# Picking by due time in the list schedule of a hybrid gMLP and attention layer

## The chip, the core and the metric

The kernel runs on one core of a Trainium2 chip. The metric is the device time of one launch in microseconds (us). Of the core's engines five matter here: the tensor engine (PE), the vector engine (DVE), the scalar engine (ACT), GpSimd (POOL), and SyncE (SP), which issues most of the DMAs. Each engine works through a list of its own in order; a semaphore makes it wait where an instruction needs what another engine or a DMA makes.

## What is computed

One layer of a streaming encoder, for two groups of tokens with the same weights: 2048 prompt tokens, and 8 running streams of 16 tokens each with 1024 cached keys and values. The width is 1024, with 4 gMLP groups and 4 attention heads of 128.

```
z = rms_norm(x, norm_g) @ w_in
u_a, v_a, g_a, q, k, v, g_b = split(z)
y_a = u_a * (tril(W_s) @ rms_norm(v_a) + b_s) * silu(g_a)      # in chunks of 128 positions
q, k = rms_norm(q), rms_norm(k)                                # two halves of 64 per head
s = q k^T / 8 - slope * |q_pos - k_pos|, block-causal with blocks of 64
o = (softmax(s of half 1) - lam * softmax(s of half 2)) @ v
y_b = rms_norm(o) * 0.8 * silu(g_b)
x = x + concat(y_a, y_b) @ w_out
```

Outputs are `x` of both groups, the new keys and values, and `v_a` of the running streams. All is float32. A product is made of three matmuls: each operand is split into a high part, rounded to a shorter format by a copy on ACT, and a low part, the difference, on DVE or POOL (`split`, line 457; `mm3`, line 469).

## The kernel before

The work has three stretches, which overlap. In the first, to about 943 us of the span, the input projection runs over blocks of weights (`stream`, line 749): for each kind and head, eight weight tiles `w` are loaded, scaled and split (`load_w`, line 608), and multiplied with the transposed tokens `xT` into PSUM accumulators `acc` (`project`, line 636). Behind each accumulator stand the copies and norms of its kind: `vo` (line 681), `z` and `qk` (656 to 674), `sg` and `usg` (688 to 701), `va`, `vn`, `vhl`, `ya` (713 to 743). They leave for DRAM. Attention of the running streams (`sample_scores`, `sample_values`) and of the first half of the prompt (`attention_a`) are woven between. In the second stretch the attention of the second half of the prompt runs together with the output projection `oo` (`out_stream`, line 1285), and in the third the last tiles of the output projection.

In attention, `score_steps` (line 869) makes scores `S` on PE, biases and reduces them on DVE (`ex`, line 889), takes the exponential on ACT (line 893) and joins both halves on DVE (line 905) or on ACT and POOL (908, 909). `value_steps` (line 913) transposes `ex` (`a_tp`), splits it (`aT`) and multiplies with `v` (`oT`). The rotated copies of the queries are made by DMAs from POOL's queue (`qT`, lines 856 and 857).

The program order written so far is not the order in which the engines work. At the end `Order(tc).run()` (line 1340) goes over all instructions and fixes each engine's list:

- `depend` (line 118) finds for each instruction which earlier ones it needs; `buffers` (line 144) finds which tiles share a buffer.
- `cost` (line 188) gives two times in ns for an instruction: until its result is there, and until its engine is free for the next.
- `port` (line 217) marks the instructions of DVE that can't run beside one of POOL.
- `run` (line 229) then plays the program on a clock of its own. An instruction becomes ready when all that it needs is done, plus a reach and a slack for the engine that waits (`SLACK`, `OTHER`, lines 68 and 69); a DMA is done after `FETCH` and its transfer. Whenever an engine is free, it takes of its ready instructions the one with the lowest number, that is, the earliest in program order (lines 321 to 330). Tiles that share a buffer keep their program order.
- What comes out (line 372) is an order per engine, for the DMA issues of SP and POOL as well. On the chip each engine follows this order and starts each instruction when its data is there.

Program order follows the use on PE: the generators yield after each few matmuls, and `weave` (line 1198) alternates them by PE time. The steps behind an accumulator stand right behind its last matmul, although what they make may be needed much later; weights stand where their load is begun.

Of the kernel before, what the change touches and what calls it, by code (L numbers as in the profile page):

```python
# [59 lines left out]
class Order:  # L60
# [4 lines left out]
    PE, ACT, DVE, POOL, SP = (mybir.EngineType.PE, mybir.EngineType.Activation, mybir.EngineType.DVE,  # L65
                              mybir.EngineType.Pool, mybir.EngineType.SP)

    SLACK = {PE: 180.0, SP: 300.0}
    OTHER, FETCH = 50.0, 2300.0

    class Node:
        def __init__(self, ins, idx):
# [115 lines left out]
    def cost(self, n):  # L188

        kind = type(n.ins).__name__[4:]  # L190
        size = max([math.prod([k for s, k in a.ap[1:]]) for a in n.reads + n.writes] or [1])
        accum = len(n.writes) > 1
        if n.dma:
            return 0.0, 560.0 if n.engine == self.POOL else 400.0
        if n.engine == self.PE:
            size = math.prod([k for s, k in n.writes[0].ap[1:]])
            t = 109.0 if size <= P else 4 + 0.4455 * size
            return t + 165, t
        if n.engine == self.ACT:
            t = 165 + 0.83 * size if kind == "TensorCopy" else 205 + 0.835 * size  # L200
            return (t + 190, t + 90) if accum else (t, t - 105)
        if n.engine == self.DVE:
            t = {"TensorTensor": 160 + 1.04 * size, "TensorReduce": 160 + 1.03 * size, "Memset": 100 + 0.5 * size,
                 "Reciprocal": 162.0}.get(kind, 205 + 1.04 * size)
            if size == 1:
                return (270.0, 190.0) if kind == "TensorScalarPtr" else (165.0, 90.0)
            if kind == "TensorScalarPtr" and not n.ins.is_scalar_tensor_tensor:
                t = 170 + 0.56 * size
            return (t + 100, t - 40) if accum else (t, t - 85)
        if kind == "Memset":  # L210
            return 100 + 0.83 * size, 100 + 0.83 * size
        if "pow" in str(n.ins):
            return 300 + 200.0 * size, 250 + 200.0 * size
        t = 190 + 2.16 * size if kind == "TensorTensor" else 195 + 1.1 * size
        return t, t - 50

    def port(self, n):

# [7 lines left out]
        large = math.prod([k for s, k in n.writes[0].ap[1:]]) >= 512 and type(n.ins).__name__ == "InstTensorScalarPtr"  # L226
        return int(len(wide) > 1 or (len(wide) == 1 and large and not psum))

    def run(self):
        N = self.nodes  # L230
        reach = {self.PE: 54.0, self.POOL: 80.0, self.SP: 27.0}
        for n in N:
            n.wait = len(n.deps)
            for d in n.deps:
                N[d].after.append(n.idx)
# [17 lines left out]
        for g in self.gates:  # L253
            for i in g[1]:
                gate[i].append(g)
            for i in g[2]:
                N[i].wait += 1
        cost = [self.cost(n) for n in N]
        ready = [0.0] * len(N)
        left = {k: len(q) for k, q in self.queue.items()}  # L260
        users = {x: len(self.uses[x]) for x in self.tag}
        last, slot, taken, freed = {}, {}, set(), {}
        free = {e: 0.0 for e in (self.POOL, self.DVE, self.ACT, self.PE, self.SP)}
        later, now_, turn, held = {e: [] for e in free}, {e: [] for e in free}, {e: [] for e in free}, set()
        port, busy = [self.port(n) for n in N], [0.0, 0.0, 0.0]
# [21 lines left out]
        def arrive(i):  # L287
            if N[i].new:
                held.add(i)
            else:  # L290
                heapq.heappush(later[N[i].engine], (ready[i], i))

        def place():
            for i in sorted(held):
                got = buffer(i)
                if got:
                    for name, s in got[1]:
                        taken.add(s)
                        slot[name] = s
                        left[s[0]] -= 1  # L300
                    ready[i] = max(ready[i], got[0])
                    held.discard(i)
                    heapq.heappush(later[N[i].engine], (ready[i], i))
                    return True
            return False
# [7 lines left out]
        while left_over:  # L313
            t, e = None, None
            for x in free:
                lock = busy[2 if x == self.DVE else 1]
                for y in ((free[x],) if now_[x] else ()) + ((max(free[x], lock),) if turn[x] else ()) + (
                        (max(free[x], later[x][0][0]),) if later[x] else ()):
                    if t is None or y < t:
                        t, e = y, x  # L320
            while later[e] and later[e][0][0] <= t:
                i = heapq.heappop(later[e])[1]
                heapq.heappush((turn if port[i] else now_)[e], i)
            lock = busy[2 if e == self.DVE else 1]
            if turn[e] and lock <= t and (not now_[e] or turn[e][0] < now_[e][0]):
                i = heapq.heappop(turn[e])
            elif now_[e]:
                i = heapq.heappop(now_[e])
            else:
                continue  # L330
            left_over -= 1
            n = N[i]
            out[e].append(i)
            if n.dma:
                size = 4 * math.prod([k for s, k in n.writes[0].ap])
                dma = max(t + self.FETCH, dma) + max(size / 280, 60.0)
                end = dma + 200
            else:
                end = t + cost[i][0]
            free[e] = t + cost[i][1]  # L340
            if port[i]:
                busy[port[i]] = free[e]
            for j in n.after:
                b = N[j].engine
                if b == e and not n.dma and not N[j].dma:
                    r = free[e]
                else:
                    r = end + reach.get(b, 35.0) + (self.SLACK.get(b, self.OTHER) if b != e or n.dma else 0)
                ready[j] = max(ready[j], r)
                N[j].wait -= 1  # L350
                if not N[j].wait:
                    arrive(j)
            more = list(first[i])
            for g in gate[i]:
                g[0] -= 1
                if not g[0]:
                    more += g[2]
            for j in more:
                ready[j] = max(ready[j], t)
                N[j].wait -= 1  # L360
                if not N[j].wait:
                    arrive(j)
            for name in n.tiles:
                if name in users:
                    last[name] = max(last.get(name, 0.0), end + 35)
                    users[name] -= 1
                    if not users[name]:
                        taken.discard(slot[name])
                        freed[slot[name]] = last[name]
            while held and place():  # L370
                pass
# [7 lines left out]
def trunk_step_kernel(  # L379
# [588 lines left out]
    def attention(sb, sl, groups, wmax, nk, nv, nex, comb, eng):  # L968
# [31 lines left out]
        for i, (key, j) in enumerate(units):  # L1000
# [33 lines left out]
            for _, run in sorted(events, key=lambda e: e[0]):  # L1034
                yield run()
# [350 lines left out]
```

## Time and profile before

| | |
|---|---|
| median of 3 runs | 1396.93 us |
| lowest and highest | 1396.93 and 1399.89 us |
| profiled execution, its own time | 1396.8 us |
| its span in the trace | 1395.0 us |
| granted PE clock over the span | 0.998 |
| matmuls | 9892 |
| DMA issues, SP and POOL queue | 991 and 96 |
| moved by DMA | 183.05 MB, mean 131 GB/s |

In the profile's rows "L627" is a line of the kernel, `out<-in` are tiles, PE is the matmul, PEld the load of its stationary operand, SPq a DMA issue on SP. A row of the timeline begins with the start in us from the start of the span and the time taken, and ends with the idle time of the engine before it and what ended that. A row of the waits has the engine and tile that waited, what it waited for, the sum in us, how often, and the longest. A row of a tile or a line has the count and the least, median and largest duration in ns. A row of the groups has the busy time in us and the mean of one in ns.

### The profile page before, as it was taken

How to read it: one execution, taken by the hardware profiler on the slowest of the kernel's cores; microseconds unless marked ns; L12 is line 12 of the kernel's file. 1: busy time of each engine (PE TensorE's matmuls, PEld its weight loads, DVE VectorE, ACT ScalarE, POOL GpSimd, SP SyncE). 2: the span in 40 equal slices, each digit the busy share in tenths (PEclk: the TensorE clock that was granted, in tenths of full speed). 3: DMA queues.
4: the chain of work that ended last, by engine and by line, in shares of the span. 5: the costliest groups of instructions: out<-in, count | busy, mean ns of one | idle time of the engine just before them, and what ended most of it. 6: DMA issues, size and time to landing. Idle time of an engine off the chain costs nothing. (4 is left out here: it accounts for less than half of the span.)

```text
span 1395.0 us, 27945 instructions
## 1 busy us (share of the span) xinstructions
PE 1355.2 (97%) x9892; PEld 1258.4 (90%) x9892; DVE 889.4 (64%) x2114; ACT 794.0 (57%) x1778; POOL 615.9 (44%) x796
## 2 busy tenths in 40 slices
PE   6999999999999999999999999999999999999998
PEld 5999999999999899999999999997788888888887
DVE  4433447765666684798887764324888887877721
ACT  5433347766565776677656553224676777676620
POOL 2261534646464565656625142023555545445400
PEclk9999999999999999999999999999999999999999
DMA  6623234544545576645533242235555444442323
GB/s 196 191 82 112 71 89 144 158 140 131 144 125 154 151 205 193 180 126 130 159 92 110 74 145 81 79 120 190 157 150 166 129 120 127 148 125 65 103 84 102
DMA packets 209244, 183.05 MB, mean 131 GB/s; under 512 B 21104, under 2 KB 167024, under 8 KB 209104
## 3 DMA queue, kind: packets, MB, share of 16 engines
q1 hardware_dynamic: 199280, 155.17, 37.9%
q0 software_dynamic: 9824, 26.09, 6.8%
q8 instruction: 78, 1.28, 0.4%
q14 instruction: 62, 0.51, 0.1%
HBM read 130.86 MB, written 42.47 MB: 124 GB/s over the span
## 5 line engine op out<-in xcount | busy, mean ns | idle before, releaser
L394 PE MATMUL acc<-w,xT 128*128 128x256 f32 x5376 | 715.2, 283 | 9.1 <-DVE w L627 3.1
L394 PEld LDWEIGHTS acc<-w,xT 128*128 128x128 f32 x5376 | 675.2, 190 | 23.2 <-DVE w L627 4.3
L394 PE MATMUL oo<-wo,yT 128*128 128x512 f32 x816 | 235.2, 401 | 1.0 <-ACT yT L459 1.0
L394 PE MATMUL S<-kT,qT 128*128 128x512 f32 (+3 forms) x688 | 184.9, 361 | 1.5 <-DMA qT<-qT 0.9
L893 ACT ACTIVATE ex<-ex,sst 128x128 f32<-128x128 f32 (+15 forms) x128 | 153.8, 1203 | 41.5 <-DVE sst L889 41.1
L394 PEld LDWEIGHTS oo<-wo,yT 128*128 128x128 f32 x816 | 146.1, 188 | 25.1 <-ACT yT L459 1.5
L394 PE MATMUL oT<-aT,v 128*128 128x256 f32 x864 | 154.6, 295 | 0.2
L627 DVE SCALAR_TENSOR_TENSOR w<-wraw,normg,w 128x256 fp32r<-128x256 f32 x224 | 119.3, 559 | 54.2 <-ACT w L626 52.9
L889 DVE CUSTOM_DVE_ANT_0 ex<-S,dist,sst 128x512 f32<-128x512 f32 (+2 forms) x192 | 123.6, 653 | 33.1 <-PE S L394 31.6
L626 ACT ACTIVATE w<-wraw,normg 128x256 fp32r<-128x256 f32 x220 | 104.3, 505 | 65.6 <-DMA wraw<-in_w_in_dram 49.1
L460 POOL TENSOR_TENSOR sv<-svraw,sv 128x512 fp32r<-128x512 f32 (+1 forms) x72 | 94.4, 1314 | 89.4 <-ACT sv L459 63.4
L394 PEld LDWEIGHTS oT<-aT,v 128*128 128x128 f32 x864 | 122.8, 190 | 6.0 <-DVE aT L460 0.8
L394 PEld LDWEIGHTS S<-kT,qT 128*128 128x128 f32 x688 | 111.8, 189 | 17.7 <-DVE sst L889 3.9
L459 ACT CAST aT<-a_tp 128x512 fp32r<-128x512 f32 (+1 forms) x144 | 79.8, 560 | 79.7 <-PE a_tp L398 78.8
L460 DVE TENSOR_TENSOR aT<-a_tp,aT 128x512 fp32r<-128x512 f32 (+1 forms) x144 | 94.0, 658 | 23.1 <-ACT aT L459 22.2
L398 PE MATMUL a_tp<-ident,ex 128*128 128x128 f32 x544 | 89.9, 276 | 5.5 <-DVE ex L905 4.1
L889 DVE CUSTOM_DVE_ANT_0 ex<-S,dist 128x512 f32<-128x512 f32 (+3 forms) x128 | 78.7, 629 | 21.0 <-PE S L394 14.8
L398 PEld LDWEIGHTS a_tp<-ident,ex 128*128 128x128 f32 x544 | 64.0, 141 | 21.2 <-issue 5.2
L1105 POOL TENSOR_TENSOR slo<-slo,dist_s 64x256 f32<-64x256 f32 (+1 forms) x64 | 50.0, 781 | 68.6 <-ACT slo L1104 63.1
L909 POOL TENSOR_TENSOR ex<-ex 128x1024 f32<-128x1024 f32 (+4 forms) x32 | 58.5, 1849 | 20.9 <-ACT ex L908 20.8
L905 DVE SCALAR_TENSOR_TENSOR ex<-ex,sst 128x1024 f32<-128x1024 f32 (+4 forms) x64 | 63.6, 1000 | 1.3
L715 POOL TENSOR_TENSOR gb<-sg,subg 128x256 f32<-128x256 f32 (+1 forms) x36 | 26.6, 738 | 82.0 <-DVE sg L690 81.7
(144 smaller groups left out, 1931.0 us busy)
## 6 DMA issues: line engine op xcount, KB each, us to landing
wraw<-in_w_in_dram SPq DMA_DIRECT2D x160, 128.0 KB, 2.7
skraw<-in_cache_k_dram SPq DMA_DIRECT2D x64, 256.0 KB, 3.1
svraw<-in_cache_v_dram SPq DMA_DIRECT2D x64, 256.0 KB, 3.0
kT<-k_scr POOLq DMA_DIRECT2D x20, 512.0 KB, 5.7
vraw<-out_dram SPq DMA_DIRECT2D x36, 256.0 KB, 2.9
y<-y_scr SPq DMA_DIRECT2D x34, 256.0 KB, 3.1
out_dram<-xo SPq DMA_DIRECT2D x34, 256.0 KB, 2.0
wraw<-in_w_in_dram SPq DMA_DIRECT2D x128, 64.0 KB, 2.5
```

What stands on the lines that cost most here:

```text
L394: pe.last = nc.tensor.matmul(*a, **k).ins
L398: pe.last = nc.tensor.transpose(*a, **k).ins
L459: act.copy(hi, src)
L460: (lo_eng or dve).tensor_tensor(out=lo, in0=src, in1=f(hi), op=ALU.subtract)
L626: act.activation(w[:, 0], r, AF.Copy, scale=normg[:, kc:kc + 1])
L627: dve.scalar_tensor_tensor(out=w[:, 1], in0=r, scalar=normg[:, kc:kc + 1], in1=f(w[:, 0]), op0=ALU.mult, op1=ALU.subtract)
L715: pool.tensor_tensor(out=gb[:, 2 * k:2 * k + m], in0=s, in1=subg.unsqueeze(1).broadcast_to([P, m, P]), op=ALU.mult)
L889: dve.tensor_tensor_reduce(out=ex[c][:, a:b], in0=s, in1=dist[:, off + a:off + b], scale=SLOPES[h], scalar=prev[c], op0=ALU.add, op1=ALU.m ...
L893: act.activation(ex[c][:, :w], ex[c][:, :w], AF.Exp, bias=prev[c], scale=-1.0, accum_out=st[:, c, 6:7])
L905: dve.scalar_tensor_tensor(out=p0, in0=p1, scalar=st[:, 1, 7:8], in1=p0, op0=ALU.mult, op1=ALU.add)
L909: pool.tensor_tensor(out=p0, in0=p1, in1=p0, op=ALU.add)
L1105: pool.tensor_tensor(out=lo, in0=lo, in1=dist_s[rh, x:x + w_], op=ALU.add)
```

## The change

Three things change in `Order`, and nothing else in the kernel. First, an instruction of any engine but PE, and each DMA, gets a due time. PE's instructions are laid end to end in program order; that gives each its time. Backwards from there, an instruction is due before the earliest due time of those that need it, less its own duration and the reach. The next user of a buffer counts as one that needs it. What nothing on PE needs is due 15 us (`LATE`) after its place in program order. Second, a free engine takes the ready instruction that is due first, where it took the earliest in program order; PE's rank is still its program order. Third, numbers of the plan's clock change: 250 ns for 180 as slack in front of PE, 2500 ns for 2300 for a fetch, 120 ns more until POOL is free for the next instruction, and an instruction that needs one before it on its own engine (DVE, POOL, ACT) is ready only after that one's end and 25, 80 or 20 ns.

```diff
-    SLACK = {PE: 180.0, SP: 300.0}
-    OTHER, FETCH = 50.0, 2300.0
+    SLACK = {PE: 250.0, SP: 300.0}
+    OTHER, FETCH, LATE = 50.0, 2500.0, 15000.0
...
         t = 190 + 2.16 * size if kind == "TensorTensor" else 195 + 1.1 * size
-        return t, t - 50
+        return t, t + 70
...
+    def deadlines(self, cost, reach):
+
+        N, t, when = self.nodes, 0.0, []
+        for n in N:
+            when.append(t)
+            if n.engine == self.PE:
+                t += cost[n.idx][1]
+        due = [x if n.engine == self.PE else x + self.LATE for n, x in zip(N, when)]
+        then = [set(n.after) for n in N]
+        for k, q in self.queue.items():
+            for a, b in zip(q, q[self.bufs[k]:]):
+                for i in self.uses[a]:
+                    then[i].add(self.uses[b][0])
+        for n in reversed(N):
+            end = self.FETCH + 600 if n.dma else cost[n.idx][0]
+            for j in then[n.idx]:
+                if j > n.idx:
+                    due[n.idx] = min(due[n.idx], due[j] - end - reach.get(N[j].engine, 35.0))
+        return [w if n.engine == self.PE else d for n, w, d in zip(N, when, due)]
+
     def run(self):
         N = self.nodes
         reach = {self.PE: 54.0, self.POOL: 80.0, self.SP: 27.0}
+        same = {self.DVE: 25.0, self.POOL: 80.0, self.ACT: 20.0}
...
+        rank = self.deadlines(cost, reach)
...
-                heapq.heappush((turn if port[i] else now_)[e], i)
+                heapq.heappush((turn if port[i] else now_)[e], (rank[i], i))
...
-                i = heapq.heappop(turn[e])
+                i = heapq.heappop(turn[e])[1]
             elif now_[e]:
-                i = heapq.heappop(now_[e])
+                i = heapq.heappop(now_[e])[1]
...
             for j in n.after:
                 b = N[j].engine
                 if b == e and not n.dma and not N[j].dma:
-                    r = free[e]
+                    r = max(free[e], end + same[e]) if e in same else free[e]
```

## The prediction

> **What bounds the kernel now.** I read the busy shares first, then the busy time by stage, then what the tensor engine (PE) waited for, and last the timeline around single waits.
>
> ```profile
> span 1395.0 us, 27945 instructions
> PE 1355.2 (97%) x9892; PEld 1258.4 (90%) x9892; DVE 889.4 (64%) x2114; ACT 794.0 (57%) x1778; POOL 615.9 (44%) x796
> ```
>
> By stage, from the start of the span; each engine's busy time stands in the order PE, weight load, DVE, ACT, POOL, and then the granted clock. Below are the first matmul and the last compute instruction.
>
> ```profile
> 0.00:50.00 50.00, 36.65 (x258) 33.67 (x258) 22.49 (x48) 25.45 (x49) 10.58 (x28) 0.97 0.74 220
> 50.00:950.00 900.00, 885.85 (x7117) 858.89 (x7117) 552.32 (x1299) 500.64 (x1252) 412.64 (x537) 1.00 0.45 130
> 950.00:1060.00 110.00, 102.74 (x591) 86.16 (x590) 85.09 (x216) 72.13 (x137) 55.79 (x70) 0.98 0.47 139
> 1060.00:1395.00 335.00, 330.00 (x1931) 279.66 (x1929) 229.51 (x554) 195.81 (x342) 136.91 (x162) 1.00 0.40 119
> 8.33 1.97 PE L398 MATMUL x_tp<-ident,x 128*128 128x128 f32 x8 [8.33 <-DVE x L583]
> 1391.31 0.69 DVE L1312 TENSOR_TENSOR xo<-oo,xo 128x512 f32<-128x512 f32 x1 [4.91 <-PE oo L394]
> ```
>
> The kernel is bound by PE: it is idle for 1395.0 - 1355.2 = 39.8 us. By stage (stretch less the PE column) that is 13.35, 14.15, 7.26 and 5.00 us. The first 8.33 us come before the first matmul, whose input is then not there, and the last 1395.0 - 1391.3 = 3.7 us come after the last one. Neither is a matter of order. What is left is 39.8 - 8.3 - 3.7 = 27.8 us of waits in the middle. The clock column is at 0.97 to 1.00, so nothing is to be had there.
>
> Now what PE waited for. The view has 22 rows; here are the largest but for the one at the start, and the last. The number after the time counts the waits, 40 over all 22 rows.
>
> ```profile
> PE a_tp L398 <- DVE ex L905: 4.1, 3, 1.8
> PE acc L394 <- DVE w L627: 3.1, 3, 1.7
> PE sO L394 <- ACT sv L459: 3.0, 5, 1.2
> ...
> PE k_tp L398 <- DVE qT L463: 0.3, 1, 0.3
> ```
>
> The restart after a wait needs two more rows: the costliest group, and a stretch in which PE was never idle.
>
> ```profile
> L394 PE MATMUL acc<-w,xT 128*128 128x256 f32 x5376 | 715.2, 283 | 9.1 <-DVE w L627 3.1 <-ACT w L626 1.8 <-ACT z L656 1.4
> 800.00:900.00 100.00, 100.00 (x835) 99.30 (x835) 49.81 (x99) 42.57 (x119) 26.56 (x38) 1.00 0.36 103
> ```
>
> The waits are scattered over many causes, each about 1 us, and most name DVE or ACT, not a DMA. A wait also costs a restart that the idle column does not count: a projection matmul is drawn as 283 ns long, but 835 of them start in a full 100 us, one per 120 ns, so the last one before a wait hides 283 - 120 = 0.16 us. For 40 waits that is 6.4 us. All that a better order could ever remove is therefore 27.8 + 6.4 = 34.2 us.
>
> **The change part by part.** No instruction is added, removed or resized. Only the order in each engine's list moves, for compute and for the DMAs of the SP and POOL queues alike. So the sum is one of waits removed less waits made.
>
> *Due time in place of program order.* Three waits show what an order can do.
>
> ```profile
> 32.35 1.06 ACT L578 ACTIVATE xsq<-x 128x1024 bf16<-128x1024 f32 x1 [2.12 <-DMA x<-in_x_prompt_dram]
> 33.41 0.57 ACT L681 COPY vo<-acc 128x512 f32<-128x512 f32 x1
> 27.81 4.19 PE L394 MATMUL acc<-w,xT 128*128 128x256 f32 x31
> 34.03 1.56 PE L394 MATMUL acc<-w,xT 128*128 128x256 f32 x11 [1.15 <-ACT vo L681]
> 246.99 0.62 ACT L459 CAST vhl<-vn 128x512 fp32r<-128x512 f32 x1 [1.48 <-DVE vn L724]
> 248.03 0.62 ACT L459 CAST sv<-svraw 128x512 fp32r<-128x512 f32 x1
> 240.01 2.27 SPq L1131 DMA_DIRECT2D svraw<-in_cache_v_dram  x2
> 248.70 0.51 PE L394 MATMUL sO<-sv,saT 128*128 128x512 f32 x1 [1.22 <-ACT sv L459]
> 762.66 0.62 ACT L459 CAST vhl<-vn 128x512 fp32r<-128x512 f32 x1 [1.07 <-DVE vn L724]
> 763.18 0.51 ACT L626 ACTIVATE w<-wraw,normg 128x256 fp32r<-128x256 f32 x1
> 764.34 0.86 PE L394 MATMUL acc<-w,xT 128*128 128x256 f32 x5 [0.77 <-DVE w L627]
> ```
>
> First: the accumulator that `vo` empties is complete at 27.81 + 4.19 = 32.00, ACT is idle until 32.35 because its list holds the square `xsq` first and that waits for a load. `vo` runs at 33.41, and PE stands for 1.15 us. With `vo` first it would end at 32.0 + 0.6 = 32.6, before PE runs out of other work at 34.03 - 1.15 = 32.88: 1.15 us gone. Second: ACT is free at 246.99 - 1.48 = 245.51 and stands 1.48 us for `vhl`, while `sv` waits behind it. Its load is the second of two issued from 240.01 on, by 242.28, and I put its landing 3.0 us later, at 245.3 (an estimate; the row is in the next fence). Taken first it ends at 246.1, and the 1.22 us go. Third: the same `vhl` holds `w` at 762.66, and the 0.77 us go. Together 3.14 us.
>
> Three others do not go.
>
> ```profile
> 185.53 0.74 PE L394 MATMUL acc<-w,xT 128*128 128x256 f32 x4 [1.38 <-ACT z L656]
> 185.11 0.37 ACT L656 COPY z<-acc 128x256 f32<-128x256 f32 x1 [0.55 <-POOL qk L667]
> 976.44 1.06 PE L398 MATMUL a_tp<-ident,ex 128*128 128x128 f32 x8 [1.85 <-DVE ex L905]
> 974.11 2.18 DVE L905 SCALAR_TENSOR_TENSOR ex<-ex,sst 128x1024 f32<-128x1024 f32 x1
> 973.95 1.26 POOL L1310 TENSOR_TENSOR xo<-yo,xo 128x512 f32<-128x512 f32 x1
> 943.98 0.97 PE L394 MATMUL oo<-wo,yT 128*128 128x512 f32 x3 [0.77 <-ACT yT L459]
> L905 DVE SCALAR_TENSOR_TENSOR ex<-ex,sst 128x1024 f32<-128x1024 f32 x24 | 32.7, 1367 | 0.6
> svraw<-in_cache_v_dram SPq DMA_DIRECT2D x64, 256.0 KB, 3.0
> ```
>
> `z` waits for a buffer that POOL still reads. `ex` is stretched from a mean of 1.37 to 2.18 us beside a POOL add that started 0.16 us earlier; an engine that is free takes the add, due or not. `yT` is a bare chain from transpose to matmul. Together 1.38 + 1.85 + 0.77 = 4.00 us.
>
> So 3.14 of 7.14 us, or 44%, go where I looked. Applied to the 34.2 us: 15 us removed. The bounds of this share are 0 and 1, that is 0 and 34 us. A wait removed is worth 3.14 / 3 + 0.16 = 1.2 us, so that is 12 of the 40.
>
> What I cannot see is what the new order makes late. Each engine stays greedy, and work of little urgency (output copies, stores, gates) may now be taken as if it were wanted 15 us later; what hides it is that a buffer's next user puts a due time on it too. On SP a store that loads pass costs PE nothing until its buffer is wanted; on POOL's queue the `qT` transfers can come to stand behind an add of 1.26 us (the `xo` row). Where the cover fails the price is a wait like the one for `z`, 1.38 + 0.16 = 1.54 us. I take four of these, 6 us: one made for three removed, a choice and not a measurement, on the low side because the rows show DVE and ACT idle just before the waits and not overrun. Its bounds are none and more than ten, 0 and over 15 us. Net 15 - 6 = 9 us.
>
> *The plan's clock.* Four edits lengthen what the plan assumes. Two of them can be checked:
>
> ```profile
> 6.68 0.19 POOL L466 TENSOR_SCALAR xst<-xst 128x1 f32<-128x1 f32 x1
> 6.95 0.57 POOL L467 TENSOR_TENSOR xst<-xst,mhalf 128x1 f32<-128x1 f32 x1
> 992.41 0.16 DVE L897 RECIPROCAL sst<-sst 128x1 f32<-128x1 f32 x1
> 992.61 0.27 DVE L898 TENSOR_SCALAR sst<-sst,neglam 128x1 f32<-128x1 f32 x1
> ```
>
> Dependent starts are 0.27 us apart on POOL and 0.20 on DVE. The old formulas give 196 - 50 = 146 ns and 90 ns, the new ones 196 + 80 = 276 and 165 + 25 = 190. So the old plan thought each dependent step about 0.1 us early; `vhl`, which held ACT in two of the three cases, is behind such a chain. These edits cost no time by themselves and are what lets the plan see those cases; I count them inside the 44%. The 70 ns more in front of PE and the 200 ns more per load only move their users down the list: nothing by themselves. The bound from both sides is one load's 0.2 us in each of 40 waits, 8 us either way, and I take 0, because a list's real start is set by the data and not by the plan.
>
> **The rivals.** *Nearly all goes:* the share is 1, and the same 40% come back as above: 34.2 x 0.6 = 20.5 us off, 1376 us. For it: no engine but PE is over 64% busy. Against: half of the waits that I looked at are not of this kind. Chance 0.11.
>
> *No change:* waits removed and made cancel, or the orders hardly differ from program order, which already follows PE's; 1397 us. For it: `z` waits for a buffer, and buffers stay as they are. Chance 0.14. The Trainium skill's page Perfetto Trace Analysis, section Optimization Strategy, says that consistent bubbles can mean too little SBUF or PSUM for the next tile; if that ruled here, order would bring nothing. Here the bubbles do not repeat at one place, so I give it little.
>
> *Slower, by DVE and POOL falling on each other:* a due-time order brings together DVE's `w`, just ahead of PE, and POOL's adds.
>
> ```profile
> L627 DVE SCALAR_TENSOR_TENSOR w<-wraw,normg,w x224: 462/480/1523, 8.6 to 920.3; 128x256 fp32r<-128x256 f32 x112
> ```
>
> A `w` takes 480 ns by its median and 1523 at most: 1.04 us for a collision. The gain of 9 us is gone when 9 more such steps stand in front of a waiting PE; 15 of the 224 give 1396.8 - 9 + 15.6 = 1403 us. For it: `ex` above. Against: the new plan books POOL 120 ns longer, so it keeps the two further apart. Chance 0.20. The Trainium skill's page SBUF — State Buffer, section Who interferes with whom, says that the instruction which issues second blocks fully until the first is done. By that rule `ex` would end at 973.95 + 1.26 + 1.37 = 976.58; the trace has 976.29 and agrees within 0.3 us.
>
> **How the numbers follow.** The profiled execution took 1396.8 us, 1.8 over its span and 0.1 under the median of the three runs, 1396.93. The forecast is 1396.8 - 9 = 1388 us, with a chance of 0.55; its own range is 1380 to 1394. With the rivals 0.11 + 0.14 + 0.20 the chances are: faster 0.55 + 0.11 = 0.66, within 0.2% (2.8 us, about what a measurement of this kernel can tell from no change) 0.14, slower 0.20. The range reaches from the larger gain, 1376, to the slower rival, 1403; beyond these ends I leave some 0.07 and 0.08.
>
> **What would show it.** PE idle falls from 39.8 to about 31 us, in the first 50 us and from 50 to 950 most of all. PE's waits for `vo`, and ACT's idle time for `vhl`, get shorter; the waits for `ex` stay. The busy sums of all engines stay within a few us. The prediction is wrong if idle time after the change is the same, or has moved behind `w` and `ex` with longer DVE steps, or if the gain lies where PE is counted busy.

## The result and the profile after

The changed kernel takes 1385.91 us, the median of four runs (1384.02 to 1389.58), beside 1396.93 us for the kernel before: a ratio of 0.9922, 95% interval 0.9896 to 0.9948. That is 11.0 us less, where 9 were forecast. The profiled execution took 1384.0 us with a span of 1382.2, so 12.8 us less than before's. It is the fastest of the four, 1.9 us below their median, so differences between the two profiles come out some 2 us too large.

The page and the stages of the changed kernel, with the columns as above; then, from the same kernel, the first and last compute, and the life of the output matmuls.

```profile
span 1382.2 us, 27962 instructions
PE 1349.0 (98%) x9892; PEld 1262.9 (91%) x9892; DVE 871.0 (63%) x2114; ACT 791.5 (57%) x1778; POOL 618.2 (45%) x796
...
0.00:50.00 50.00, 34.55 (x233) 33.40 (x234) 22.73 (x50) 25.41 (x49) 11.00 (x29) 0.93 0.72 220
50.00:950.00 900.00, 889.64 (x7156) 866.03 (x7155) 538.77 (x1298) 500.22 (x1254) 415.10 (x537) 1.00 0.45 130
950.00:1060.00 110.00, 106.61 (x630) 89.73 (x629) 89.31 (x235) 77.59 (x147) 60.86 (x78) 1.00 0.52 154
1060.00:1382.20 322.20, 318.25 (x1878) 273.76 (x1876) 220.17 (x534) 188.31 (x330) 131.26 (x155) 1.00 0.40 117
...
7.29 1.94 PE L420 MATMUL x_tp<-ident,x 128*128 128x128 f32 x8 [7.29 <-DMA ident<-in_c_ident_dram]
1378.53 0.69 DVE L1334 TENSOR_TENSOR xo<-oo,xo 128x512 f32<-128x512 f32 x1 [4.91 <-PE oo L416]
...
L416 PE MATMUL oo<-wo,yT x816: 387/394/502, 941.2 to 1378.1; 128*128 128x512 f32 x164
```

The same row of the kernel before is:

```profile
L394 PE MATMUL oo<-wo,yT x816: 387/394/505, 944.0 to 1390.9; 128*128 128x512 f32 x164
```

PE is idle for 1382.2 - 1349.0 = 33.2 us instead of 39.8. By stage that is 15.45, 10.36, 3.39 and 3.95 us, where it was 13.35, 14.15, 7.26 and 5.00: the first 50 us have become worse, the rest better. The `oo` rows measure two stretches by work instead of by time. The first `oo` starts 944.0 - 941.2 = 2.8 us earlier. From there to the last it takes 436.9 us instead of 446.9. So 10 of the 12.8 us were won in the last third, with attention beside the output projection. Some 2 of them are the granted clock, 1.00 for 0.98 in the row from 950 to 1060 us (0.02 x 110 = 2.2 us).

What PE waited for after the change, largest first, and the last row; the view has 17 rows with 25 waits, where before it had 22 with 40:

```profile
PE x_tp L420 <- DMA ident<-in_c_ident_dram: 7.3, 1, 7.3
PE acc L416 <- DVE w L649: 4.1, 3, 2.3
PE acc L416 <- ACT w L648: 2.6, 2, 2.2
PE x_tp L420 <- DVE neglam L474: 2.6, 1, 2.6
PE x_tp L420 <- DVE x L605: 2.2, 1, 2.2
...
PE a_tp L420 <- DVE ex L927: 1.1, 2, 0.8
...
PE sO L416 <- ACT sv L481: 1.0, 1, 1.0
...
PE oT L416 <- ACT aT L481: 0.2, 1, 0.2
```

The wait for `vo` is gone, and so is the one for `z`, 1.4 us before; `sv` went from 3.0 to 1.0 us, and `ex` from 4.1 to 1.1. New at the start is a wait of 2.6 us under the name of `neglam`, a constant that no matmul near it needs. The rows of ACT, DVE and PE around it show what it really waits for:

```profile
21.02 1.06 ACT L600 ACTIVATE xsq<-x 128x1024 bf16<-128x1024 f32 x1 [3.62 <-DMA x<-in_x_prompt_dram]
23.12 0.75 DVE L605 TENSOR_SCALAR x<-x,xst 128x1024 f32<-128x1024 f32 x1 [0.66 <-POOL xst L489]
23.79 0.15 DVE L474 TENSOR_SCALAR neglam<-neglam 128x1 f32<-128x1 f32 x1
24.02 1.07 PE L420 MATMUL x_tp<-ident,x 128*128 128x128 f32 x8 [2.56 <-DVE neglam L474]
```

The matmul reads `x`, which DVE finishes at 23.12 + 0.75 = 23.87; `neglam` only ends last, 0.07 us later. In front of `x` stands its square on ACT, which waited 3.62 us for a load. It is the fifth square, and the fifth load of `x` is issued at 13.53, behind eight small loads of constants (the rows under "The first 50 us"). So this is a wait for a load of the tokens that came late into SP's list.

### The profile page after: what moved, and what is told of

Read it like the earlier page. It is cut to its first block, busy times and chain, and to the rows that moved or that the text cites. A ratio compares the mean times of both kernels' runs of the same rounds, so it can differ in the third digit from the quotient of the medians.

```text
span 1382.2 us, 27962 instructions
## 1 busy us (share of the span) xinstructions
PE 1349.0 (98%) x9892; PEld 1262.9 (91%) x9892; DVE 871.0 (63%) x2114; ACT 791.5 (57%) x1778; POOL 618.2 (45%) x796
## 4 chain that ended last, share of the span: by engine, by line
PE 90%; ACT 3%; DMA 3%; DVE 2%; issue 1%; SPq 1%; POOL 0%; ACTq 0%; DVEq 0%
PE acc L416 45%; PE oo L416 13%; PE S L416 9%; PE oT L416 7%; PE a_tp L420 4%; PE sS L416 2%; PE sO L416 2%; PE sk_tp L420 2%; PE y_tp L420 1%; PE x_tp L420 1%; PE mix L416 1%; DVE w L649 1%; PE k_tp L420 1%; PE o_tp L420 1%; PE q_tp L420 0%
## 5 line engine op out<-in xcount | busy, mean ns | idle before, releaser
L416 PE MATMUL oo<-wo,yT 128*128 128x512 f32 x816 | 231.5, 400 | 1.0 <-ACT yT L481 1.0
L649 DVE SCALAR_TENSOR_TENSOR w<-wraw,normg,w 128x256 fp32r<-128x256 f32 x224 | 113.3, 534 | 62.4 <-ACT w L648 61.4
L416 PE MATMUL oT<-aT,v 128*128 128x256 f32 x864 | 150.5, 293 | 0.2 <-ACT aT L481 0.2
L482 DVE TENSOR_TENSOR skT<-sk_tp,skT 128x512 fp32r<-128x512 f32 x64 | 43.8, 689 | 36.1 <-ACT skT L481 35.7
L482 POOL TENSOR_TENSOR v<-vraw,v 128x512 fp32r<-128x512 f32 x36 | 46.9, 1304 | 39.2 <-ACT v L481 37.6
```

Of the source, the lines that this page charges most:

```text
L416: pe.last = nc.tensor.matmul(*a, **k).ins
L482: (lo_eng or dve).tensor_tensor(out=lo, in0=src, in1=f(hi), op=ALU.subtract)
L649: dve.scalar_tensor_tensor(out=w[:, 1], in0=r, scalar=normg[:, kc:kc + 1], in1=f(w[:, 0]), op0=ALU.mult, op1=ALU.subtract)
```

## The experiments

All kernels below compute the whole layer; only `Order` differs. Each was timed beside the kernel before, and its ratio is to that. Differences of edits are against the changed kernel unless it is said otherwise.

**Due times or the plan's clock.** My theory was that the due times make the gain and the numbers only help; the rival was that the better clock makes it. First the due times with the four old numbers:

```diff
-    SLACK = {PE: 250.0, SP: 300.0}
-    OTHER, FETCH, LATE = 50.0, 2500.0, 15000.0
+    SLACK = {PE: 180.0, SP: 300.0}
+    OTHER, FETCH, LATE = 50.0, 2300.0, 15000.0
...
-        return t, t + 70
+        return t, t - 50
...
-                    r = max(free[e], end + same[e]) if e in same else free[e]
+                    r = free[e]
```

> Due times on all engines but PE, with the four numbers of the plan's clock as they were before. Theory A (the due-time pick makes the gain, the clock numbers only help): about 1389 us, most of the 11 us gained. Theory B (the plan's clock makes the gain, since it no longer thinks dependent steps 0.1 us early): about 1396 us, no gain over the kernel before.

Measured: 1395.68 us, ratio 1.0003 (0.9991 to 1.0015). The due times alone bring nothing; theory A fails. Then the new numbers with program order:

```diff
-        rank = self.deadlines(cost, reach)
+        rank = list(range(len(N)))
```

> The four new numbers of the plan's clock, with the pick by program order as before. Theory A: 1394 to 1397 us, little or no gain. Theory B: about 1387 us, most of the gain. If both this and the due times alone fall short by much, the two need each other.

Measured: 1412.42 us, ratio 1.0113 (1.0100 to 1.0126). Theory B fails too: the better clock alone makes the kernel 16 us slower. The two need each other, which I had only named as an aside.

**Which engines.** One kernel has due times on SP alone, one on all but SP.

```diff
         rank = self.deadlines(cost, reach)
+        rank = [r if n.engine == self.SP else n.idx for n, r in zip(N, rank)]
```

> The change, but only SP, that is most DMA issues, picks by due time; ACT, DVE and POOL pick by program order. Theory C (the order of the loads is what counts, as PE's waits before named loads behind ACT's): within 3 us of the full change, about 1387 us. Theory A (the compute engines' order counts, as in the three waits of the prediction): about the same as the new clock numbers alone, 1394 to 1397 us.

Measured: 1406.02 us, ratio 1.0071 (1.0056 to 1.0086). Neither number was met: it is 6 us better than the clock with program order, but far from the change.

```diff
         rank = self.deadlines(cost, reach)
+        rank = [n.idx if n.engine == self.SP else r for n, r in zip(N, rank)]
```

> The change, but SP picks by program order; ACT, DVE and POOL pick by due time. Theory A: within 2 us of the full change, 1384 to 1388 us. Theory C: 1394 us or more. In the first 50 us PE should then be idle for some 13 us as before, not 15.5 as in the change, since the small loads of constants would again stand behind the weights.

Measured: 1386.95 us, ratio 0.9932 (0.9920 to 0.9944). The compute engines' order carries the gain, as theory A had it. SP's order adds nothing on the whole. Two stages and the output matmuls of this kernel:

```profile
0.00:50.00 50.00, 35.65 (x258) 33.61 (x258) 21.81 (x49) 25.53 (x49) 11.04 (x28) 1.00 0.71 220
...
950.00:1060.00 110.00, 103.80 (x591) 89.93 (x590) 86.04 (x225) 74.75 (x139) 55.15 (x72) 0.94 0.48 140
...
L417 PE MATMUL oo<-wo,yT x816: 387/394/502, 937.6 to 1381.6; 128*128 128x512 f32 x164
```

With SP in program order the first `oo` comes at 937.6, 3.6 us before the change's 941.2. From there it takes 1381.6 - 937.6 = 444.0 us, 7.1 more than the change. It looks as if SP by due time lost 3.6 us in the projection and won 7.1 behind it. But these are two single executions, and the granted clock differs in both places: in the first 50 us it is 1.00 here and 0.93 in the change, and from 950 to 1060 us 0.94 here and 1.00 in the change, which is 0.06 x 110 = 6.6 us of full clock. By their medians the two kernels are 1.0 us apart. So the rows do not show that the order of the loads made either part. In the first 50 us PE is idle for 50 - 35.65 = 14.35 us, not quite the 13 expected, but less than the change's 15.45.

**Which numbers.** The four numbers fall into two pairs: the steps (POOL's 120 ns, and the same-engine steps) and the margins (PE's slack and the fetch). Each pair was put beside the due times alone, with the lines of the first diff for the other pair.

> Due times, with two of the four clock edits: POOL's 120 ns and the same-engine steps; the slack in front of PE and the fetch are as before. Theory A2 (due times pay only where the plan's clock has dependent steps right): about 1387 us, like the full change. Theory D (any small change of the plan's numbers gives another order, and the time falls by chance within some 10 us): anywhere from 1384 to 1400 us.

Measured: 1386.53 us, ratio 0.9927 (0.9909 to 0.9945): the whole gain.

> Due times, with the other two clock edits: 250 ns in front of PE and 2500 ns for a fetch; POOL's and the same-engine steps are as before. Theory A2: about 1395 us, as with due times and the old clock. Theory E (the margins are what makes due times pay, since PE then puts other work in front of what comes late): about 1387 us.

Measured: 1400.06 us, ratio 1.0029 (1.0014 to 1.0043): none of it, and 4 us slower than before. Theory A2 holds, E fails.

**Is it chance?** Any change of a number gives another order, so each of these results could be luck. Two kernels move numbers by a trifle:

```diff
-    SLACK = {PE: 250.0, SP: 300.0}
-    OTHER, FETCH, LATE = 50.0, 2500.0, 15000.0
+    SLACK = {PE: 245.0, SP: 300.0}
+    OTHER, FETCH, LATE = 50.0, 2490.0, 15000.0
```

> The full change with two numbers moved so little that no theory gives it a meaning: 245 ns in place of 250 in front of PE, 2490 ns in place of 2500 for a fetch. Theories A2 and E: within 2 us of the change, 1384 to 1388 us. Theory D: off by up to 10 us either way.

Measured: 1383.71 us, ratio 0.9909 (0.9890 to 0.9928), 0.3 us below the range. And the kernel before, with 185 for 180 and 2310 for 2300:

> The kernel before with the same two numbers moved by as little: 185 ns for 180, 2310 for 2300. Theories A2 and E: within 2 us of the kernel before. Theory D: off by up to 10 us either way; then single kernels say little of single edits, and only the mean over several can.

Measured: 1397.05 us, ratio 1.0004 (0.9989 to 1.0018). Both stay within some 2 us of their neighbours, so theory D fails for moves of this size. Two such moves are few, so I read differences of about 10 us between single kernels as effects, and differences of 2 or 3 us not at all.

**Which step.** Due times and old margins, with one of the two steps.

> Due times with one clock edit: POOL is free 120 ns later after each instruction. Theory F (what counts is that an instruction that needs one before it on its own engine is ready only after that one's end, about 0.1 us later than the old plan thought): 1393 to 1398 us, as with the old clock. Theory G (what counts is POOL's time, and with it when DVE may run beside it): about 1387 us.

Measured: 1395.44 us, ratio 0.9993 (0.9983 to 1.0003).

> Due times with one clock edit: the same-engine steps. Theory F: about 1387 us. Theory G: 1393 to 1398 us. If both this and POOL's edit give some 1391 us, each has its half.

Measured: 1389.3 us, ratio 0.9955 (0.9940 to 0.9971). So the same-engine step does most of it, some 7 of 10 us, and POOL's time nothing by itself (the granted clock of that kernel's executions was lower, 0.991 to 0.994 beside 0.995 to 0.999, so what its order alone is worth is not clear). Theory F holds but for some 3 us that need both, which is about the size that chance can make. The edit holds for DVE, POOL and ACT at once; they were not tried apart. The kernels so far fall into two groups, which speaks against chance too: the five with due times on the compute engines and the same-engine steps take 1383.7 to 1389.3 us, the three with due times and without these steps 1395.4 to 1400.1.

What this step does can be seen in DVE's list. Before, the plan held a dependent instruction ready as soon as its engine took the next one, so it always followed its producer at once and DVE did nothing else in between; the rows at 992.41 in the prediction are such a pair. Counted in the traces, the multiply that needs a reciprocal comes right behind it in 72 of 72 places before, in 67 with due times and the old clock, in 50 with the same-engine step, and in 47 in the change. With these steps and program order it is 34 of 72 in the kernel of 1412.42 us, and 32 in the one of the next paragraph, which are slower than the kernel before. So to part such pairs is not the gain; it depends on what is put between, and that these places are what removes PE's waits is argued here, not shown. From DVE's timeline in the changed kernel:

```profile
1009.07 0.16 DVE L919 RECIPROCAL sst<-sst 128x1 f32<-128x1 f32 x1
1009.14 0.73 DVE L911 CUSTOM_DVE_ANT_0 ex<-S,dist,sst 128x512 f32<-128x512 f32 x1
1009.80 0.08 DVE L911 DVE_READ_ACCUMULATOR2_ANT sst<- 128x1 f32 x1
1009.80 0.27 DVE L920 TENSOR_SCALAR sst<-sst,neglam 128x1 f32<-128x1 f32 x1
```

An independent reduction starts 0.07 us behind the reciprocal, inside its recorded 0.16, while a dependent multiply stood 0.20 behind it. The Trainium skill's page Perfetto Trace Analysis, section Per-instruction lifecycle, says that the recorded end is the write's acknowledgement and that the next instruction may begin to fetch before it. This trace agrees: the reduction starts 0.07 us into a recorded 0.16.

**Why the steps alone hurt.** They were then run with program order and the old margins.

> Program order with POOL's 120 ns and the same-engine steps, slack and fetch as before. The new clock with program order took 1412 us. Theory H (right steps hurt program order, since a step that is ready later leaves the engine to an instruction with a low number and little urgency): 1408 us or more. Theory I (the margins hurt it): about 1396 us.

Measured: 1405.6 us, ratio 1.0073 (1.0053 to 1.0093), of the sign that H has, though short of its 1408; the margins add the rest to 1412. Theory I fails. One place shows what happens. From the timelines of ACT, DVE and PE in this kernel, and its first and last `oo`:

```profile
837.97 1.14 ACT L481 CAST wo<-woraw 128x512 fp32r<-128x512 f32 x2 [1.58 <-DMA woraw<-in_w_out_dram]
839.11 0.51 ACT L648 ACTIVATE w<-wraw,normg 128x256 fp32r<-128x256 f32 x1
836.42 1.77 DVE L482 TENSOR_TENSOR wo<-woraw,wo 128x512 fp32r<-128x512 f32 x1
838.11 0.82 DVE L746 SCALAR_TENSOR_TENSOR vn<-va,vst,sgug 128x128 f32<-128x128 f32 x1
839.14 1.47 DVE L482 TENSOR_TENSOR wo<-woraw,wo 128x512 fp32r<-128x512 f32 x1 [0.21 <-ACT wo L481]
840.54 1.26 DVE L649 SCALAR_TENSOR_TENSOR w<-wraw,normg,w 128x256 fp32r<-128x256 f32 x3
841.06 1.22 PE L416 MATMUL acc<-w,xT 128*128 128x256 f32 x4 [2.42 <-DVE w L649]
...
L416 PE MATMUL oo<-wo,yT x816: 387/394/504, 957.1 to 1397.8; 128*128 128x512 f32 x164
```

ACT and DVE split the output weights `wo`, which no matmul reads before 957.1, while PE stands for 2.42 us for the `w` behind them; this kernel chooses by number. In the changed kernel PE is never idle in this stretch:

```profile
825.00:860.00 35.00, 35.00 (x298) 34.88 (x297) 20.48 (x35) 18.41 (x45) 14.36 (x14) 1.00 0.57 175
```

Nor was it in the kernel before, although its order was by number too. That longer steps open more places where another instruction can get in between, and that the number then lets in the wrong one, fits both; that this is what costs all of the 9 us is argued and not shown.

There is another part, which I had overlooked: such a wait can cost more than its own time. The two stretches behind it, from the same kernel; the third number from the end is the granted clock:

```profile
841.00:844.40 3.40, 3.34 (x15) 3.34 (x16) 2.27 (x7) 1.70 (x3) 0.73 (x1) 0.50 0.88 296
844.40:860.00 15.60, 15.60 (x132) 15.47 (x131) 8.69 (x15) 6.10 (x14) 4.45 (x4) 1.00 0.46 144
```

For 3.4 us PE is granted half its clock, and 15 matmuls take 3.34 us, one per 0.22, where 132 then take 15.60, one per 0.12. That is some 1.6 us on top of the 2.42. The kernel with all new numbers and program order (1412.42 us) has the most of this. From its page:

```profile
PE 1365.2 (97%) x9892; PEld 1271.0 (90%) x9892; DVE 871.1 (62%) x2114; ACT 793.2 (56%) x1778; POOL 618.4 (44%) x796
```

With a span of 1411.5 us its PE is idle for 46.3 us, 6.5 more than before, and counted busy for 1365.2, 10.0 more, with the same 9892 matmuls. Its granted clock over the span is 0.988 where it was 0.998. So more of its 16 us lies in matmuls that run slower than in waits. It is no accident of one execution: the granted clock is 0.986 to 0.989 in the four of that kernel, 0.989 to 0.993 in the six of the one with the steps alone, and 0.995 to 0.999 in the 17 of the kernel before beside each. Not every wait has such a stretch behind it, a wait of 2.02 us at 36.43 in the last kernel below has none, and what decides it is open.

**The first 50 us.** SP's issues in the changed kernel:

```profile
9.61 0.47 SPq L548 DMA_DIRECT2D qkg<-in_q_norm_g_dram  x1
...
13.53 0.35 SPq L593 DMA_DIRECT2D x<-in_x_prompt_dram  x1
14.41 0.33 SPq L464 DMA_DIRECT2D subg<-in_subln_g_dram  x1
14.79 3.98 SPq L553 DMA_DIRECT2D bias_s<-in_sgu_b_dram  x4
...
22.87 0.43 SPq L574 DMA_DIRECT2D ws<-in_sgu_w_dram  x1
23.41 1.47 SPq L634 DMA_DIRECT2D wraw<-in_w_in_dram  x3
```

Small loads of constants fill SP's list from 9.61 on, four of `bias_s` occupy it for 3.98 us, and the next weights are issued at 23.41. In the kernel before they were issued at 14.89:

```profile
14.89 1.30 SPq L612 DMA_DIRECT2D wraw<-in_w_in_dram  x3
```

A due time doesn't forbid this: a free engine takes what is ready, however late it is due. So a load that nothing holds was made to wait until 20 us ahead of its due time:

```diff
-        ready = [0.0] * len(N)
+        ready = [max(0.0, r - 20000.0) if n.dma and n.engine == self.SP and not n.deps else 0.0
+                 for n, r in zip(N, rank)]
```

> The full change, but a load on SP that needs nothing before it isn't ready until 20 us ahead of its due time, so that the small loads of constants are out of the first 50 us. If it is these loads that cost the change some 3 us of its first 50 us (15.5 us of PE idle for 13.4 before; with SP by program order 14.4), about 1382 us, better than the change by 2 to 4 us, with PE idle for 13 us or less in the first 50 us. If not, 1386 us and the same idle time.

Measured: 1378.1 us, ratio 0.9869 (0.9855 to 0.9884), the fastest of all: 7.8 us below the change, whose interval begins above this one's end. The same rows of this kernel:

```profile
11.11 1.52 SPq L594 DMA_DIRECT2D x<-in_x_prompt_dram  x2
14.74 1.30 SPq L635 DMA_DIRECT2D wraw<-in_w_in_dram  x3
...
0.00:50.00 50.00, 37.09 (x277) 35.52 (x278) 23.66 (x48) 26.66 (x52) 11.25 (x29) 1.00 0.62 186
...
L417 PE MATMUL oo<-wo,yT x816: 387/394/504, 933.4 to 1369.9; 128*128 128x512 f32 x164
```

The weights are issued at 14.74 instead of 23.41, PE is idle for 12.9 us in the first 50 instead of 15.45, and the first `oo` comes at 933.4, 7.8 us earlier. From there it takes 436.5 us, as in the change. I had expected 2 to 4 us. The first block of 64 matmuls that run without a break stands in PE's timeline of this kernel and in that of the changed one:

```profile
24.39 7.84 PE L417 MATMUL acc<-w,xT 128*128 128x256 f32 x64
```

```profile
29.41 9.52 PE L416 MATMUL acc<-w,xT 128*128 128x256 f32 x64
```

It starts 5.0 us earlier and is done 6.7 us earlier, because the granted clock differs as well. The same stretch in this kernel and in the changed one:

```profile
26.40:33.30 6.90, 6.90 (x64) 6.90 (x62) 3.28 (x9) 2.58 (x7) 1.51 (x4) 1.00 0.39 119
```

```profile
26.40:33.30 6.90, 6.04 (x28) 6.04 (x29) 5.82 (x11) 4.34 (x9) 1.80 (x4) 0.51 0.91 267
```

By 50 us this kernel has run 277 matmuls, the changed one 233 and the kernel before 258. At 0.12 us each, an estimate from the prediction's full stretch, it is there 5.3 us ahead of the change and 2.3 ahead of the kernel before. So some 5 of the 7.8 us come from the start, and 3 of these only win back what the change had lost there. The others were won in the projection; by which load, and how much by the granted clock (0.998 to 1.000 in its four executions, 0.994 to 0.996 in the change's), is open.

## Why the prediction was right, and where it was not

**The number.** 1388 us was forecast and 1385.9 measured. The sign and the size hold, but the size partly by luck: it came out of a sum whose parts did not hold.

**The cause.** The step that failed is "These edits cost no time by themselves". The plan's numbers cost or bring more than the order does: with program order the new ones cost 16 us, with due times the two steps bring 9 of the 11. The distances that I quoted for them, 0.27 and 0.20 us between dependent starts, are what the old plan lacked, and I used them only as a remark. What I left out is that a dependent instruction which the plan holds ready 0.1 us later lets it choose another one in between, a reduction of 0.73 us in the rows at 1009.14, and that the rule of choice then decides whether this helps or harms. The other half of that sentence holds: the plan's clock is what lets due times work.

**The share of waits that go.** All three waits that were to go went. For `sv`, PE has no wait from 27.26 to 262.51 in the changed kernel. For `vo`, in ACT's timeline of the changed kernel the bracket names its accumulator, for which ACT stood idle, so nothing was ahead of it:

```profile
35.31 0.59 ACT L703 COPY vo<-acc 128x512 f32<-128x512 f32 x1 [3.02 <-PE acc L416]
```

For the `w` at 764.34, PE is never idle in this stretch of the changed kernel:

```profile
710.00:940.00 230.00, 230.00 (x1876) 226.39 (x1876) 137.14 (x340) 114.00 (x332) 73.08 (x131) 1.00 0.38 107
```

The row of `acc` on DVE's `w` rose all the same, from 3.1 to 4.1 us, by waits at other places. Of the three that were to stay, two did not. `z` went whole, so a wait for a buffer was a matter of order after all. The `ex` of 1.85 us fell to 0.8: it took 1.29 us instead of 2.18, since POOL's next subtraction began 0.86 us behind it and not in front of it. Only `yT` stayed, at 0.77 us. So 3.14 + 1.38 + 1.05 = 5.57 of the 7.14 us went, 78% where I had said 44%.

**The sum.** Waits in the middle fell from 27.8 to 33.2 - 7.3 - 3.7 = 22.2 us, and by 15 in number, 15 x 0.16 = 2.4 us of restarts. That is 8.0 us, close to the forecast of 9, but by other terms. In the first 50 us the waits behind the first matmul rose from 13.35 - 8.33 = 5.0 to 15.45 - 7.29 = 8.2 us; after that they fell from 22.8 to 14.0. The first matmul came 1.0 us earlier, which I had held to be no matter of order, and the remaining 12.8 - 9.0 = 3.8 us lie where PE is counted busy, which I had named as a sign of being wrong. What made those is open; about half may be that the profiled execution was a fast one, and the granted clock over the span is no reason, 0.996 after 0.998. Of waits made, my 6 us stood for buffers like `z`'s; what the rows show is the start, with 3.1 us. And the price of a wait left out the granted clock. I read its column, 0.97 to 1.00 by stage, as nothing to be had, but it changes with the order: the wait of 2.42 us above cost some 1.6 us more by it.

**The place.** I expected the first 50 us and the projection to gain most. The first 50 us lost 2.1 us, and 10 of 12.8 us were won behind the projection.

**The rivals.** DVE and POOL did not fall on each other more. The same rows of the changed kernel:

```profile
L649 DVE SCALAR_TENSOR_TENSOR w<-wraw,normg,w 128x256 fp32r<-128x256 f32 x224 | 113.3, 534 | 62.4 <-ACT w L648 61.4
...
L927 DVE SCALAR_TENSOR_TENSOR ex<-ex,sst 128x1024 f32<-128x1024 f32 x24 | 31.4, 1310 | 0.3
```

A `w` takes 534 ns in the mean instead of 559, `ex` 1310 instead of 1367. But that is not the gain: with program order and the new steps DVE's busy time was as low (869.8 us), and the kernel 9 us slower. The rule on buffers from the Trainium skill's page Perfetto Trace Analysis, section Optimization Strategy, did not decide: buffers stayed as they were, and the time fell, with the wait for `z`'s buffer among those that went.

## What to carry to other kernels

A list schedule is only as good as its clock: before the rule of choice is changed, compare the plan's distance between dependent instructions on one engine with the trace. A better clock and a better rule may each be worth nothing or less alone, so try them together and apart, with a small move of the numbers as a control. A due time only sorts what is ready; here it paid to hold back loads that were due much later. And read the granted clock behind the waits, stretch by stretch: a wait can be followed by some microseconds at half the clock, which no list of waits shows.

## What the runs showed of the hardware

A DVE instruction that needs the one before it starts 0.20 us behind a one-column reciprocal, while an independent one can start 0.07 us behind it. Behind some of PE's waits the granted clock is 0.50 for 3.4 us, and matmuls start 0.22 us apart instead of 0.12; it was so behind a wait of 2.42 us. On SP's queue the issue of a small load of a constant costs as much as that of a tile of weights: 0.47 us for `qkg` and 1.30 / 3 = 0.43 us for `wraw` in the rows above. In the changed kernel 19 such loads and two of `x` stand between 9.61 and 23.41 us, ahead of the next weights; why the first four `bias_s` took 3.98 us was not tried.
